# A grouped 3x3 convolution on one core: weight masks made between the first and second load issue, first loads in half images, later ones in whole images

## The chip, the cores and the metric

The kernel runs on one core of a Trainium2 chip. The metric is the device time of one execution in microseconds (us); of several executions the median counts. TensorE is PE in the profile, its weight load PEld, VectorE DVE, ScalarE ACT, GpSimd POOL, SyncE SP. Sixteen DMA engines move data between HBM and the core.

## The reference

x is float32 of 16 images, 64 channels, 64x64 pixels. The 64 input channels fall into 8 groups of 8, the 128 output channels into 8 groups of 16, and a 3x3 kernel with a border of zeros runs within each group. The output is float32, 16 x 128 x 64 x 64.

```python
x_pad = np.pad(x, ((0, 0), (0, 0), (pad, pad), (pad, pad)), mode='constant')
for g in range(groups):
    for b in range(batch):
        for co in range(c_out_per_group):
            for ci in range(c_in_per_group):
                for kh in range(k):
                    for kw in range(k):
                        output[b, g * c_out_per_group + co] += \
                            weight[g * c_out_per_group + co, ci, kh, kw] * \
                            x_pad[b, g * c_in_per_group + ci, kh:kh+h, kw:kw+w]
```

## The kernel before

Data. x is read as 1024 rows (image, channel) of 4096 pixels. Four tiles `xn[i]` and four tiles `xs[i]`, 128 rows each, hold all of it as bf16, so that each has its own place and no load ever waits for a tile to come free. `xn[i]` starts at row 128i and holds two whole images; `xs[i]` starts at row 544 + 128i, shifted by half an image, so that 32 of its rows belong to the group before or after: 32 rows of `xs[3]` (rows 96 to 127) hold the first half of image 8 and are needed in group 0. `load` (L52 to L56) issues one DMA on GpSimd's queue that reads float32 and writes bf16. The tile framework gives the loads eight semaphores in turn, so the ninth load waits on POOL until the first has landed, the tenth until the second, and so on.

Order of the loads (L61 to L69). Group 0 (`xn[0]`, the 32 rows of `xs[3]`, `xs[0]`) comes in three cuts of image rows: 0 to 16, 16 to 32, 32 to 64. Groups 1 to 3 come in two halves of 32 image rows for `xn[i]` and `xs[i]`. These are 21 DMAs. A 128-row half is 1 MB as read, a quarter 512 KB.

Weights. `w_sb` (36 KB) is loaded on SP's queue (L59). DVE sets `mask` to one and `ident` to zero (L74, L84); POOL makes of them, by three affine selects (L75, L79, L85), the mask of 8 groups and the identity. They stand behind all loads in POOL's order. DVE multiplies `w_sb` with `mask` into `E` (L94, five instructions), PE transposes `E` by 18 matmuls with `ident` (L107), and DVE and ACT copy the results as bf16 into `wN` and `wS` (L115, L117): block-diagonal weights for 32 input channels by 64 output channels at a time.

The main loop. Four groups i, each of four images; in each, eight chunks c of 8 image rows. For a chunk, four PSUM tiles of 128 x 512 are filled by 9 taps times 8 streams, 72 matmuls of 32 rows by 64 columns (`mm`, L131), each with its own weight load; eight PSUM tiles let two chunks be open. DVE and ACT in turn copy each PSUM tile into an output tile `ob` (L161, L163). After four chunks, SP issues four stores of 1 MB (L168), one for each image's half. Sixteen `ob` tiles, so four such sets, are in use before one is written again. Chunk 3 reads one image row beyond the first half (the tap below), so chunks 0 to 2 need the first 32 rows alone.

Of the kernel before, what the change touches and what calls it, by code (L numbers as in the profile page):

```python
# [7 lines left out]
FP32 = mybir.dt.float32  # L8
BF16 = mybir.dt.bfloat16
ALU = mybir.AluOpType  # L10
# [3 lines left out]
def kernel(  # L14
# [7 lines left out]
    nc = tc.nc  # L22

    B, C, H, W = x.shape
    CO, CIg, K, _ = weight.shape
    G = groups
    COg = CO // G
# [8 lines left out]
    wpool = ctx.enter_context(tc.tile_pool(name="wpool", bufs=1))  # L36
# [9 lines left out]
    xn = [xpool.tile([128, H, W], BF16, name=f"xn{i}") for i in range(4)]  # L46
    xs = [xpool.tile([128, H, W], BF16, name=f"xs{i}") for i in range(4)]

    def flat(t):
        return t.rearrange("p h w -> p (h w)")  # L50

    def load(t, row0, p0, p1, h0, h1):  # L52
        nc.gpsimd.dma_start(  # L53
            flat(t)[p0:p1, h0 * W : h1 * W],
            xr[row0 + p0 : row0 + p1, h0 * W : h1 * W],
        )  # L56
# [1 line left out]
    w_sb = wpool.tile([128, CIg * T], FP32)  # L58
    nc.sync.dma_start(w_sb, weight.rearrange("co ci kh kw -> co (ci kh kw)"))  # L59

    cuts = [0, 16, 32, 64]  # L61
    for h0, h1 in zip(cuts, cuts[1:]):
        load(xn[0], 0, 0, 128, h0, h1)
        load(xs[3], 512 - 96, 96, 128, h0, h1)
        load(xs[0], 544, 0, 128, h0, h1)
    for i in range(1, 4):
        for h0, h1 in ((0, 32), (32, 64)):
            load(xn[i], 128 * i, 0, 128, h0, h1)
            load(xs[i], 544 + 128 * i, 0, 128 if i < 3 else 96, h0, h1)  # L69

    mask = wpool.tile([128, G], FP32)
    nc.vector.memset(mask, 1.0)  # L74
    nc.gpsimd.affine_select(  # L75
        out=mask, in_=mask, compare_op=ALU.is_ge, fill=0.0,
        base=0, channel_multiplier=1, pattern=[[-COg, G]],
    )
    nc.gpsimd.affine_select(  # L79
        out=mask, in_=mask, compare_op=ALU.is_ge, fill=0.0,  # L80
        base=COg - 1, channel_multiplier=-1, pattern=[[COg, G]],
    )
    ident = wpool.tile([128, 128], BF16)
    nc.vector.memset(ident, 0.0)  # L84
    nc.gpsimd.affine_select(  # L85
        out=ident, in_=ident, compare_op=ALU.not_equal, fill=1.0,
        base=0, channel_multiplier=1, pattern=[[-1, 128]],
    )
    E = wpool.tile([128, T, 160], BF16)
    wv = w_sb.rearrange("co (ci t) -> co t ci", t=T)  # L90
    ge = 160 // CIg
# [112 lines left out]
```

## Time and profile before

| what | us |
|---|---|
| median of 3 executions | 147.95 |
| lowest and highest | 146.76, 151.19 |
| the profiled execution | 146.28 |
| its span, first to last instruction | 144.5 |
| PE busy | 77.0 |
| DVE busy | 45.7 |
| ACT busy | 37.1 |
| POOL busy | 12.0 |

The span is what the trace shows of the profiled execution. Its mean granted TensorE clock is 0.908 of 2.4 GHz. Matmuls of different rows and columns of the array run beside each other, so a matmul's own duration is not its share of the time.

### The profile page before, as it was taken

How to read it: one execution, taken by the hardware profiler on the slowest of the kernel's cores; microseconds unless marked ns; L12 is line 12 of the kernel's file. 1: busy time of each engine (PE TensorE's matmuls, PEld its weight loads, DVE VectorE, ACT ScalarE, POOL GpSimd, SP SyncE). 2: the span in 40 equal slices, each digit the busy share in tenths (PEclk: the TensorE clock that was granted, in tenths of full speed). 3: DMA queues.
4: the chain of work that ended last, by engine and by line, in shares of the span. 5: the costliest groups of instructions: out<-in, count | busy, mean ns of one | idle time of the engine just before them, and what ended most of it. 6: DMA issues, size and time to landing. Idle time of an engine off the chain costs nothing.

```text
span 144.5 us, 4928 instructions
## 1 busy us (share of the span) xinstructions
PE 77.0 (53%) x2322; PEld 51.5 (36%) x2322; DVE 45.7 (32%) x74; ACT 37.1 (26%) x68; POOL 12.0 (8%) x28
## 2 busy tenths in 40 slices
PE   0000000049966954769792993899549499930000
PEld 0000000045733632646571672566336367620000
DVE  0000000191534526117373333355603336613000
ACT  3000000003533524214352232254503325502000
POOL 6733312300000000000000000000000000000000
PEclk9999999999999999779999699599986869999655
DMA  3999999999997996995199799749999925998991
GB/s 41 118 185 214 215 215 210 213 214 217 215 206 219 426 426 277 413 410 245 75 428 413 290 426 413 295 168 401 426 426 422 415 91 211 404 426 367 428 424 75
DMA packets 7444, 42.29 MB, mean 293 GB/s; under 512 B 992, under 2 KB 992, under 8 KB 3328
## 3 DMA queue, kind: packets, MB, share of 16 engines
q1 hardware_dynamic: 4752, 33.59, 56.0%
q0 software_dynamic: 2672, 8.39, 30.4%
q8 instruction: 18, 0.29, 0.8%
q14 instruction: 2, 0.02, 0.0%
HBM read 16.81 MB, written 33.55 MB: 348 GB/s over the span
## 4 chain that ended last, share of the span: by engine, by line
PE 53%; issue 17%; DMA 16%; DVE 2%; POOL 2%; DVEq 0%; POOLq 0%
PE ps L131 52%; DMA xs<-in_x_dram 11%; DMA xn<-in_x_dram 5%; DVE E L94 2%; PE ps L107 1%; POOL xn L53 1%; POOL xs L53 1%; DVE ob L163 0%; DVEq L199 0%; POOL ident L85 0%; POOL mask L75 0%; POOLq L199 0%; POOLq L75 0%; POOLq L185 0%
## 5 line engine op out<-in xcount | busy, mean ns | idle before, releaser
L131 PE MATMUL ps<-xs,wS 32*64 32x504 bf16 (+3 forms) x1152 | 73.7, 412 | 22.6 <-issue 22.4
L131 PE MATMUL ps<-xn,wN 32*64 32x504 bf16 (+3 forms) x1152 | 74.9, 413 | 0.0
L163 DVE COPY ob<-ps 128x512 f32<-128x512 f32 x64 | 41.2, 686 | 57.5 <-PE ps L131 57.5
L131 PEld LDWEIGHTS <-wS 32*64 32x64 bf16 x1152 | 47.3, 115 | 18.6 <-issue 3.1
L161 ACT COPY ob<-ps 128x512 f32<-128x512 f32 x64 | 34.6, 589 | 63.1 <-PE ps L131 54.3
L131 PEld LDWEIGHTS <-wN 32*64 32x64 bf16 x1152 | 40.3, 115 | 29.1 <-issue 27.8
L107 PE MATMUL ps<-ident,E 128*128 128x128 bf16 x18 | 2.1, 313 | 30.8 <-DVE E L94 30.8
L107 PEld LDWEIGHTS <-E 128*128 128x128 bf16 x18 | 1.8, 147 | 30.8 <-DVE E L94 30.8
L94 DVE TENSOR_TENSOR E<-w_sb,mask 128x288 bf16<-128x288 f32 x5 | 2.9, 643 | 27.4 <-POOL mask L79 27.4
L117 ACT CAST wS<-ps 128x512 bf16<-128x512 f32 (+1 forms) x3 | 1.2, 487 | 30.3 <-PE ps L107 30.3
L53 POOL DMA_DIRECT2D xs<-in_x_dram x12 | 6.4, 536 | 9.9 <-DMA xs<-in_x_dram 7.3
L53 POOL DMA_DIRECT2D xn<-in_x_dram x9 | 5.0, 550 | 6.0 <-DMA xn<-in_x_dram 4.6
L115 DVE CAST wN<-ps 128x512 bf16<-128x512 f32 (+1 forms) x3 | 1.5, 551 | 0.1
L117 ACT ACT_TABLE_LOAD x1 | 1.3, 1283 | 0.8 <-PEq L185 0.8
L74 DVE MEMSET mask<- 128x8 f32 x1 | 0.1, 65 | 0.9 <-PEq L185 0.9
L85 POOL TENSOR_SCALAR_AFFINE_SELECT ident<-ident 128x128 bf16<-128x128 bf16 x1 | 0.3, 298 | 0.0
L75 POOL TENSOR_SCALAR_AFFINE_SELECT mask<-mask 128x8 f32<-128x8 f32 x1 | 0.2, 204 | 0.1
L79 POOL TENSOR_SCALAR_AFFINE_SELECT mask<-mask 128x8 f32<-128x8 f32 x1 | 0.2, 191 | 0.0
L185 POOL MEMSET const-float32-0.0<- 128x1 f32 x1 | 0.1, 99 | 0.3 <-issue 0.3
L84 DVE MEMSET ident<- 128x64 uint32 x1 | 0.1, 112 | 0.0
L185 POOL MEMSET const-bfloat16-1.0<- 128x1 bf16 x1 | 0.1, 102 | 0.0
L185 POOL MEMSET const-uint8-127<- 128x1 uint8 x1 | 0.1, 102 | 0.0
(1 smaller groups left out, 0.1 us busy)
## 6 DMA issues: line engine op xcount, KB each, us to landing
out_dram<-ob SPq DMA_DIRECT2D x32, 1024.0 KB, 8.8
xn<-in_x_dram POOLq DMA_DIRECT2D x7, 512.0 KB, 17.6
xs<-in_x_dram POOLq DMA_DIRECT2D x5, 512.0 KB, 16.2
xs<-in_x_dram POOLq DMA_DIRECT2D x2, 384.0 KB, 19.4
xn<-in_x_dram POOLq DMA_DIRECT2D x2, 256.0 KB, 5.8
xs<-in_x_dram POOLq DMA_DIRECT2D x2, 256.0 KB, 6.9
xs<-in_x_dram POOLq DMA_DIRECT2D x2, 64.0 KB, 5.7
xs<-in_x_dram POOLq DMA_DIRECT2D x1, 128.0 KB, 9.5
```

Of the source, the lines that this page charges most:

```text
L53: nc.gpsimd.dma_start(flat(t)[p0:p1, h0 * W : h1 * W], xr[row0 + p0 : row0 + p1, h0 * W : h1 * W],)
L75: nc.gpsimd.affine_select(out=mask, in_=mask, compare_op=ALU.is_ge, fill=0.0, base=0, channel_multiplier=1, pattern=[[-COg, G]],)
L79: nc.gpsimd.affine_select(out=mask, in_=mask, compare_op=ALU.is_ge, fill=0.0, base=COg - 1, channel_multiplier=-1, pattern=[[COg, G]],)
L85: nc.gpsimd.affine_select(out=ident, in_=ident, compare_op=ALU.not_equal, fill=1.0, base=0, channel_multiplier=1, pattern=[[-1, 128]],)
L94: nc.vector.tensor_mul(E[:, :, 32 * r : 32 * r + 32].rearrange("p t (g c) -> p t g c", c=CIg), wv.unsqueeze(2).to_broadcast([128, T, 4, CIg]),
L107: nc.tensor.matmul(ps[:, 128 * t : 128 * t + 128], E[:, t0 + t, off : off + 128], ident, start=True, stop=True,)
L115: nc.vector.tensor_copy(dst, ps[:, 0 : 128 * n])
L117: nc.scalar.copy(dst, ps[:, 0 : 128 * n])
L131: nc.tensor.matmul(d3[64 * half : 64 * half + 64, o0 : o0 + nr, v0 : v0 + nw], wt[32 * q : 32 * q + 32, 3 * kh + kw, 64 * half : 64 * half ...
L161: nc.scalar.copy(dst, pcs[b])
L163: nc.vector.tensor_copy(dst, pcs[b])
L185: nc = _bacc.Bacc("TRN2", target_bir_lowering=False, num_devices=1)
```

## The change

The masks' memsets and the three selects move up. POOL now issues the first load, runs the selects, and then issues the other loads. Group 0 comes in two halves instead of three cuts, with `xs[0]` before the piece of `xs[3]`; groups 1 to 3 come as whole images, one DMA for each tile. There are 12 loads instead of 21. All that follows (`E`, the transposes, the main loop, the stores) is the same.

```diff
-    cuts = [0, 16, 32, 64]
-    for h0, h1 in zip(cuts, cuts[1:]):
+    mask = wpool.tile([128, G], FP32)
+    ident = wpool.tile([128, 128], BF16)
+    nc.vector.memset(mask, 1.0)
+    nc.vector.memset(ident, 0.0)
+
+    def make_masks():
+        nc.gpsimd.affine_select(
+            out=mask, in_=mask, compare_op=ALU.is_ge, fill=0.0,
+            base=0, channel_multiplier=1, pattern=[[-COg, G]],
+        )
...
+    for h0, h1 in ((0, 32), (32, 64)):
         load(xn[0], 0, 0, 128, h0, h1)
+        if h0 == 0:
+            make_masks()
+        load(xs[0], 544, 0, 128, h0, h1)
         load(xs[3], 512 - 96, 96, 128, h0, h1)
-        load(xs[0], 544, 0, 128, h0, h1)
     for i in range(1, 4):
-        for h0, h1 in ((0, 32), (32, 64)):
-            load(xn[i], 128 * i, 0, 128, h0, h1)
-            load(xs[i], 544 + 128 * i, 0, 128 if i < 3 else 96, h0, h1)
...
-    nc.gpsimd.affine_select(
...
+        load(xn[i], 128 * i, 0, 128, 0, H)
+        load(xs[i], 544 + 128 * i, 0, 128 if i < 3 else 96, 0, H)
```

POOL before, the last loads and what follows them (names carry a running number; DMASW0 to DMASW7 are the semaphores of the loads):

```order
L53 DMA xn3_70<-in_x_dram 128x2048 [waits DMASW3_49]
L53 DMA xs3_74<-in_x_dram 96x2048 [waits DMASW4_49]
L75 ISA
L75 AFFINE_SELECT mask_98<-mask_98 128x8 [waits DVE_49]
L85 AFFINE_SELECT ident_102<-ident_102 128x128 [waits DVE_49]
L79 AFFINE_SELECT mask_98<-mask_98 128x8 [waits Pool_49]
L199 UNCONDITIONAL_BRANCH
```

POOL of the changed kernel, from the first load to the second that waits:

```order
L53 DMA xn0_67<-in_x_dram 128x2048
L67 ISA
L67 AFFINE_SELECT mask_77<-mask_77 128x8 [waits DVE_49]
L75 AFFINE_SELECT ident_78<-ident_78 128x128 [waits DVE_49]
L71 AFFINE_SELECT mask_77<-mask_77 128x8 [waits Pool_49]
L53 DMA xs0_71<-in_x_dram 128x2048
L53 DMA xs3_74<-in_x_dram 32x2048
L53 DMA xn0_67<-in_x_dram 128x2048
L53 DMA xs0_71<-in_x_dram 128x2048
L53 DMA xs3_74<-in_x_dram 32x2048
L53 DMA xn1_68<-in_x_dram 128x4096
L53 DMA xs1_72<-in_x_dram 128x4096
```

The selects stood behind 21 loads, 13 of which wait for an earlier one to land; now one load stands ahead of them, and it waits for none.

PE before, at chunk 3 of group 1, where the matmuls first touch the second half of `xn[1]` and `xs[1]` (PE's first matmul of the group, further up, waits for the first half, DMASW1 and DMASW2):

```order
L131 MATMUL ps_1047<-xs0_71,wS_114 64x8x63
L131 LDWEIGHTS wN_113
L131 MATMUL ps_1045<-xn1_68,wN_113 64x8x63 [waits DMASW3_49]
L131 LDWEIGHTS wS_114
L131 MATMUL ps_1047<-xs1_72,wS_114 64x8x63 [waits DMASW4_49]
```

PE of the changed kernel at the beginning of group 1:

```order
L134 MATMUL ps_710<-xs3_74,wS_105 64x7x63
L134 LDWEIGHTS wN_104 [waits DMASW6_49]
L134 MATMUL ps_796<-xn1_68,wN_104 64x512 [waits Activation_49]
L134 LDWEIGHTS wS_105 [waits DMASW7_49]
L134 MATMUL ps_798<-xs1_72,wS_105 64x512 [waits DVE_49]
```

The waits of chunk 3 are gone, and the group's first matmuls wait for the whole tiles, the seventh and eighth load (DMASW6, DMASW7). PE's instructions are otherwise the same, 4646 in both.

## Rows read from the trace of the kernel before

**Rows 1.** The page: busy tenths in 40 slices of the span, and GB/s.
```profile
PE   0000000049966954769792993899549499930000
...
DMA  3999999999997996995199799749999925998991
GB/s 41 118 185 214 215 215 210 213 214 217 215 206 219 426 426 277 413 410 245 75 428 413 290 426 413 295 168 401 426 426 422 415 91 211 404 426 367 428 424 75
```

**Rows 2.** Chain of waits: start us, us, what; the first row by engine.
```profile
PE 53%; issue 17%; DMA 16%; DVE 2%; POOL 2%; DVEq 0%; POOLq 0%
...
28.40 2.32 DVE E L94 x4
...
41.91 3.66 PE ps L131 x128
...
47.01 3.66 PE ps L131 x128
...
58.58 5.29 PE ps L131 x128
...
65.05 3.66 PE ps L131 x128
...
69.60 7.12 PE ps L131 x256
...
130.34 0.68 DVE ob L163
```

**Rows 3.** Timeline of POOL and SP: start us, us, instruction, idle before it.
```profile
0.81 0.38 SPq L59 DMA_DIRECT2D w_sb<-in_weight_dram  x1
1.29 0.67 POOL L53 DMA_DIRECT2D xn<-in_x_dram  x1 [0.78 <-POOLq L185]
...
27.18 0.52 POOL L53 DMA_DIRECT2D xs<-in_x_dram  x1 [1.93 <-DMA xs<-in_x_dram]
27.79 0.20 POOL L75 TENSOR_SCALAR_AFFINE_SELECT mask<-mask 128x8 f32<-128x8 f32 x1
...
28.18 0.19 POOL L79 TENSOR_SCALAR_AFFINE_SELECT mask<-mask 128x8 f32<-128x8 f32 x1
...
44.94 89.98 SPq L168 DMA_DIRECT2D out_dram<-ob  x32
```

**Rows 4.** Timeline of PE from 30 us.
```profile
30.77 2.10 PE L107 MATMUL ps<-ident,E 128*128 128x128 bf16 x18 [30.77 <-DVE E L94]
...
33.98 0.63 PE L131 MATMUL ps<-xs,wS 32*64 32x512 bf16 x2
```

**Rows 5.** Busy time by stretch, with PEclk, DMA share, GB/s at the end.
```profile
48.90:53.00 4.10, 2.39 (x95) 1.50 (x80) 1.77 (x3) 1.16 (x3) 0.00 (x0) 1.00 1.02 424
68.40:70.80 2.40, 1.51 (x64) 0.90 (x55) 0.65 (x2) 0.51 (x2) 0.00 (x0) 1.00 0.03 10
...
142.80:144.55 1.75, 0.00 (x0) 0.00 (x0) 0.00 (x0) 0.00 (x0) 0.00 (x0) 0.50 0.00 0
```

**Rows 6.** DMA queues: packets, MB, share; the page, then 44.8:45.8, 50:51, 62.6:63.6.
```profile
q8 instruction: 18, 0.29, 0.8%
...
HBM read 16.81 MB, written 33.55 MB: 348 GB/s over the span
...
q8 instruction: 1, 0.02, 6.0%
...
q8 instruction: 1, 0.02, 5.5%
...
q8 instruction: 1, 0.02, 5.8%
```

**Rows 7.** DMA issues, KB as written, us to landing; the last row: stores (tile ob).
```profile
xn<-in_x_dram POOLq DMA_DIRECT2D x2, 256.0 KB, 5.8
...
w_sb<-in_weight_dram SPq DMA_DIRECT2D x1, 36.0 KB, 1.9
...
DMA to landing us min/median/max: 4.2/8.8/12.1
```

More of the change, by code (lines that the diff above doesn't have):

```diff
@@ L59 @@
     nc.sync.dma_start(w_sb, weight.rearrange("co ci kh kw -> co (ci kh kw)"))
-    cuts = [0, 16, 32, 64]
-    for h0, h1 in zip(cuts, cuts[1:]):
+    mask = wpool.tile([128, G], FP32)
[7 more added lines that the diff above has]
+        )
+        nc.gpsimd.affine_select(
+            out=mask, in_=mask, compare_op=ALU.is_ge, fill=0.0,
+            base=COg - 1, channel_multiplier=-1, pattern=[[COg, G]],
+        )
+        nc.gpsimd.affine_select(
+            out=ident, in_=ident, compare_op=ALU.not_equal, fill=1.0,
+            base=0, channel_multiplier=1, pattern=[[-1, 128]],
+        )
+    for h0, h1 in ((0, 32), (32, 64)):
         load(xn[0], 0, 0, 128, h0, h1)
+        if h0 == 0:
+            make_masks()
+        load(xs[0], 544, 0, 128, h0, h1)
         load(xs[3], 512 - 96, 96, 128, h0, h1)
-        load(xs[0], 544, 0, 128, h0, h1)
     for i in range(1, 4):
-        for h0, h1 in ((0, 32), (32, 64)):
-            load(xn[i], 128 * i, 0, 128, h0, h1)
-            load(xs[i], 544 + 128 * i, 0, 128 if i < 3 else 96, h0, h1)
-    mask = wpool.tile([128, G], FP32)
-    nc.vector.memset(mask, 1.0)
-    nc.gpsimd.affine_select(
[L76 to L88, printed above, removed]
+        load(xn[i], 128 * i, 0, 128, 0, H)
+        load(xs[i], 544 + 128 * i, 0, 128 if i < 3 else 96, 0, H)
     E = wpool.tile([128, T, 160], BF16)
```

## The prediction

> **What bounds the kernel now.** I read the page's busy shares and its forty slices first [rows 1], then the chain of waits in order of time [rows 2], then POOL's and the first PE instructions [rows 3, 4], and last the DMA engines by stretch and queue [rows 5 to 7].
>
> The slices fall into two phases [rows 1]. Through the first eight slices PE does nothing while the DMA row stands at 9; after that PE works and the DMA row has holes. The span is 144.5 us, the profiled execution took 146.28 us, so 1.78 us lie around the span; the median of the three runs, 147.95 us, is 1.67 us above that execution. I sum against 146.28.
>
> Why PE idles to 30.77 us: POOL issues the loads and also makes the masks, and the masks come last. From the ninth load on, each issue waits for an earlier load to land (1.93 us at the last one); the last load goes out at 27.18 us, the three mask instructions run from 27.79 to 28.37, DVE starts E at 28.40 and PE its first matmul at 30.77 [rows 3, 4]. The weights and the first images were there long before: loads of 256 KB as written, 512 KB as read, landed 5.8 us after issue [rows 7].
>
> Why PE then takes from 33.98 us (the first matmul on xs, where the stream becomes dense [rows 4]) to 130.34 us [rows 2]: 128 matmuls in a row take 3.66 us, then comes a gap (1.44 us from 41.91 + 3.66 = 45.57 to 47.01) that the chain gives to "issue", 17% of the span in all, so nothing that the profile shows released it [rows 2]. The step of 128 tells what is missing: 128 matmuls and 128 weight loads are 256 instructions, and the instruction queue moved 18 packets of 0.29 MB in all, 16 KB each [rows 6], which is 64 bytes for each of 256. So PE waits for its next block of program. The places agree: a whole instruction packet (5.5 to 6.0% of 16 engines' 1 us, about 0.9 us) lies in 44.8:45.8, in 50:51 and in 62.6:63.6 [rows 6], and PE resumes at 47.01 and 65.05 [rows 2], 1.2 and 1.5 us behind the first and the last of these stretches. With the DMA busy, the packet in 50:51 begins 3.0 us after the resumption at 47.01 and that in 62.6:63.6 begins 4.0 us after the one at 58.58. Where the DMA is nearly idle (68.4:70.8, share 0.03 [rows 5]) the next block boundary has no gap: 256 matmuls run in one piece from 69.60 [rows 2]. From 41.91 to 69.60 are five such cycles, 5.54 us each; the whole dense stage is 96.4 us for 18 blocks, 5.35 each. The program supply, slowed by data transfers, paces PE; PE paces the stores; the DMA idles at times.
>
> The DMA's own floor: stores run at 424 GB/s, loads show 214 because what is written is half of what is read [rows 1, 5], so both move some 426 GB/s at their wider end. 16.81 MB read and 33.55 MB written [rows 6] are then 39.4 + 78.8 = 118.2 us; one 1 MB load or store is 2.46 us.
>
> **The change, part by part.** Masks: the three POOL instructions, 0.6 us, move from behind 21 loads to behind the first one. The first issue ends at 1.29 + 0.67 = 1.96 us [rows 3], the masks at about 2.65; the weight load lands at 0.81 + 1.9 = 2.7 us [rows 3, 7]. E's 2.32 us of lead [rows 2] then end at 5.0 us, PE can begin at 5.1, and its first matmul on images, behind the 2.10 us of weight matmuls [rows 4], at 7.2. The memsets that the masks need stay DVE's first instructions. The 0.6 us by which the second load is later costs nothing: the first load, now 1 MB, gives the DMA 2.46 us of work.
>
> What is late next is the data: two 1 MB halves and the quarter piece, 2.46 + 2.46 + 0.62 = 5.5 us from about 2.6 us on, where the DMA starts (the first slice of 3.6 us is 0.3 busy [rows 1]), so 8.1 us. A landing adds to that; the shortest store took 4.2 us for 2.46 us of transfer [rows 7], so 0 to 1.7, and I take 0.9. The dense stream begins at 9.0 us instead of 33.98: **25.0 us earlier**. If all behind it kept its pace, the span would be 119.5 us.
>
> Whole images instead of halves: PE now waits at the first chunk of group 1 for all of both tiles, not half. Group 0 is 11.1 us of loads, to 13.7; group 1 adds 9.84, to 23.5 us alone. PE comes to group 1 after 576 matmuls, 4.5 cycles of 5.54 us, at 9 + 25 = 34 us. The stores begin (first issue 44.94 [rows 3], 11.0 us after the dense start) at 20.0 us and halve the rate for the rest, so group 1 lands near 28. Group 2 at half rate lands at 48, wanted at 59 or later; group 3 at 66, wanted at 84. Cost nothing; with only a third of the rate for loads group 3 lands near 88, so up to 4 us. The two row cuts in group 0 merge with no wait: chunk 3 needs the second half at about 19 us, it lands at 14.5. Fewer, larger DMAs also take the slow start away (118 and 185 GB/s in the second and third slice, 214 after [rows 1]): some 2 us less DMA time, free unless the DMA bounds.
>
> What it gives back: loads and stores now overlap, which no stretch of before shows; the stores began at 44.94 us [rows 3], and GB/s goes there from the loads' 214 to the stores' 426 within two slices [rows 1]. At 20.0 us, 17.4 of the loads' 39.4 us are done and 22.0 left; at half the rate that is 44 us, at two thirds 33; I take 38.5 us of mixed traffic. In it a program block has two data queues to get past. Bounds for its extra wait: 0 (the wait is the same with one queue or two) and 4.92 us (one whole-image load of 2 MB at full rate, ahead of it each time). I take 2.46 us, one 1 MB transfer, since the waits seen with one queue, 3.0 and 4.0 us, are of that size. Cycle 5.54 + 2.46 = 8.0 us, 38.5/8.0 = 4.8 cycles, **11.8 us later**. Upper bound: 44/10.46 = 4.2 cycles, 20.7 us. Below nothing I see no way, as the DMA is never emptier than before.
>
> A rule bears on this by itself. The Trainium skill, DMA: Bandwidth & Descriptors, section Queues, rings and completion order, says that each DMA engine takes its queues in turn and drains a whole packet, typically 9 to 17 descriptors, before it switches. By that rule a second busy queue adds one turn to each fetch; its size for whole images would be the upper bound above, and the span 119.5 + 20.7 + 2.1 = 142.3 us. The 3.0 and 4.0 us measured beside one queue fit a turn of about 2.5 us, and no row here has two.
>
> After the loads the DMA is backlogged all the time, with no idle stretch such as 68.4:70.8 in which a block comes in time. I charge the five-cycle mean instead of the stage's: 0.19 us for each of about 11 cycles, **2.1 us**.
>
> Sum: 144.5 - 25.0 + 11.8 + 2.1 = 133.4 us of span, 135.2 us with the 1.78 around it. Check against the DMA: 2.6 + 118.2 + 1.7 (the empty end, 142.8 to 144.5 [rows 5]) = 122.5 us, so PE and its program still bound, by 11 us, and the end stays as it is, four stores behind PE's last matmul.
>
> **The rivals.** (a) The program fetch is not slowed by a second queue: 119.5 + 2.1 is under the DMA's 122.5, so the DMA bounds, 122.5 to 127 us of span, 124 to 129 us. For it: a packet's own 0.9 us is the same as the loads end (44.8:45.8) and amid stores (62.6:63.6) [rows 6]. Against: the gap goes where the DMA empties. A rule of the Trainium skill ends here too: Runtime: NRT & Kernel Launch, section Instruction fetch mechanics, has the crossing of a 16 KiB program block mostly hidden. By it PE would run through and the DMA's floor would decide; the gaps in the chain, 17% of the span, speak against it.
>
> (b) Each fetch waits for whole-image loads, the upper bound: 119.5 + 20.7 + 2.1 = 142.3, minus what a PE that stalls gives back (fewer stores, so the loads end sooner): 138 to 142 us, 140 to 144 with what lies around. The large packets speak for it.
>
> (c) Slower: loads and stores in flight together run at a lower joint rate. About 44 us of DMA work (22 of loads, as much of stores) is mixed. The time passes 150.9 us, 2% over 147.95, when the span passes 149.1, 26.6 over the floor: 44/r - 44 = 26.6, r = 0.62, some 265 GB/s together. From there it decides; at r = 0.6 the span is 151.8, 153.6 us with the rest. Nothing in the trace has the two together, for or against; stores alone reach 424 and loads, counted as read, 428.
>
> (d) Hardly any gain (145 to 151 us): r near 0.66, or loads that get so little of the DMA that groups 2 and 3 starve PE by 10 us on top of (b). That the masks don't come early is no case: the order of POOL's instructions shows them second.
>
> **How the numbers follow.** Forecast (129 to 140) 0.52, (a) 0.22, (b) 0.16, (d) 0.06, (c) 0.04. The range 126 to 143 leaves out the lower part of (a), (c), (d) and the end of (b), 2 in 10. A measurement of this kernel tells about 2%; faster by more than that means under 145.0: 0.90 from the forecast, (a) and (b). Within 2%: 0.06. Slower: 0.04.
>
> **What would show it.** Right: masks done before 3 us, first matmul near 5, dense stream near 9; program gaps longer between 20 and 60 us (cycles near 8 us) than after; group boundaries with no wait on DMA; PE's last matmul 13 us before the end. Wrong: a DMA row full from start to end with GB/s at 426 (then a), a joint rate clearly under 400 while both queues are busy (c or d), matmuls released by xn or xs at group 2 or 3, or cycles of 8 us that go on after the loads.

## The result, and the profile after

| | before | after |
|---|---|---|
| median, us | 147.35 (4 runs) | 132.66 (4 runs, 132.49 to 132.89) |
| profiled execution, us | 146.28 | 132.79 |
| its span, us | 144.5 | 131.1 |

The ratio of after to before is 0.900, 95% interval 0.894 to 0.906. The forecast was 135.2 us, within 126 to 143.

The head of the program, as the timeline of the changed kernel has it (start us, us, instruction), from POOL, DVE and PE:

```profile
1.30 0.66 POOL L53 DMA_DIRECT2D xn<-in_x_dram  x1 [0.79 <-POOLq L188]
2.05 0.21 POOL L67 TENSOR_SCALAR_AFFINE_SELECT mask<-mask 128x8 f32<-128x8 f32 x1
...
2.44 0.19 POOL L71 TENSOR_SCALAR_AFFINE_SELECT mask<-mask 128x8 f32<-128x8 f32 x1
...
2.75 2.88 DVE L97 TENSOR_TENSOR E<-w_sb,mask 128x288 bf16<-128x288 f32 x5 [1.72 <-DMA w_sb<-in_weight_dram]
...
5.12 2.10 PE L110 MATMUL ps<-ident,E 128*128 128x128 bf16 x18 [5.12 <-DVE E L97]
7.21 2.98 PE L134 MATMUL ps<-xn,wN 32*64 32x512 bf16 x13
10.13 0.64 PE L134 MATMUL ps<-xs,wS 32*64 32x512 bf16 x2
```

Against [rows 3, 4]: the masks end at 2.63 us instead of 28.37, and E now waits for the weight load. PE's stream gets dense at 10.13 us instead of 33.98, 23.85 us earlier. The page's slices, beside [rows 1]:

```profile
PE   0499997497546556587919884759749289340000
...
DMA  3999999999999999999999999999999729989991
GB/s 31 173 209 211 230 210 223 200 293 273 290 280 295 270 295 268 395 423 420 425 415 428 420 415 423 428 420 418 400 415 420 295 118 420 423 343 393 435 423 48
```

The holes of the DMA row are gone but for one, at 104 to 107 us. PE's row has more of them. The chain of waits (start us, us, what), beside [rows 2]:

```profile
24.80 5.35 PE ps L134 x128
...
30.99 3.56 PE ps L134 x119
...
37.74 3.61 PE ps L134 x128
...
43.93 3.66 PE ps L134 x128
...
50.40 3.66 PE ps L134 x128
...
56.32 5.25 PE ps L134 x124
...
98.60 3.66 PE ps L134 x128
102.26 3.08 issue
105.34 7.12 PE ps L134 x256
...
116.90 0.68 DVE ob L166
```

Stretches (duration, then busy us of each engine; the last two numbers are the DMA share and GB/s), and the two data queues while both run, in 28:48 (packets, MB, share):

```profile
24.80:50.40 25.60, 16.18 (x512) 10.95 (x512) 9.02 (x14) 7.62 (x14) 0.00 (x0) 0.93 1.02 279
56.32:104.00 47.68, 33.96 (x1024) 22.05 (x1024) 18.05 (x28) 15.13 (x28) 0.00 (x0) 0.89 1.00 415
104.00:106.70 2.70, 1.36 (x56) 1.00 (x63) 0.52 (x1) 0.67 (x2) 0.00 (x0) 1.00 0.23 85
```

```profile
q0 software_dynamic: 383, 2.79, 66.6%
q1 hardware_dynamic: 389, 2.82, 34.8%
```

So the span went from 144.5 to 131.1 us in three terms. The start came 23.85 us earlier. The dense stage got longer, from 96.4 to 106.8 us (10.13 to 116.90): 10.4 us given back. Behind PE's last matmul stand 14.2 us, as before. What the stage pays is the cycle of 128 matmuls, one program block: 5.35 us on average before; now 6.40 while loads and stores overlap (four cycles from 24.80 to 50.40) and 6.13 under stores alone (eight from 56.32 to 105.34). The queue rows say that the overlap itself is cheap: 2.79 MB written are 5.58 MB read, so 8.4 MB moved in 20 us, 420 GB/s, close to either alone [rows 1, 5].

Neither the clock nor the matmuls set the length of these cycles. Two stretches of PE, and the program packet (queue q8) that begins in 41.6:41.7:

```profile
24.80:30.14 5.34, 5.34 (x128) 3.37 (x128) 1.95 (x4) 1.89 (x4) 0.00 (x0) 0.68 0.96 264
...
37.74:41.35 3.61, 3.61 (x128) 2.76 (x128) 1.29 (x2) 1.07 (x2) 0.00 (x0) 1.00 1.03 281
```

```profile
q8 instruction: 1, 0.02, 58.4%
```

In the first the granted clock was 0.68 on average, part of it at 1.2 GHz, behind 2.81 us in which PE had no matmul. In the second it was at 2.4 GHz. The 128 matmuls took 5.34 and 3.61 us, the gaps behind them 0.85 and 2.58 us, and both cycles are 6.19 us long (24.80 to 30.99, 37.74 to 43.93). The packet begins 3.9 us after PE resumed at 37.74, takes 0.93 us (58.4% of 16 engines' 0.1 us), and PE goes on 1.4 us behind its end.

### The profile page after: what moved, and what is told of

Its sections match the earlier page's. It is cut to its first block, busy times and chain, and to the rows that moved or that the text cites. A ratio compares the mean times of both kernels' runs of the same rounds, so it can differ in the third digit from the quotient of the medians.

```text
span 131.1 us, 4919 instructions
## 1 busy us (share of the span) xinstructions
PE 79.4 (61%) x2322; PEld 52.4 (40%) x2322; DVE 45.8 (35%) x74; ACT 37.1 (28%) x68; POOL 7.2 (6%) x19
## 4 chain that ended last, share of the span: by engine, by line
PE 61%; issue 25%; DVE 2%; DMA 1%; DVEq 0%
PE ps L134 59%; DVE E L97 2%; PE ps L110 2%; DMA w_sb<-in_weight_dram 1%; DVE ob L166 1%; DVEq L202 0%; DVEq L97 0%
## 5 line engine op out<-in xcount | busy, mean ns | idle before, releaser
L134 PE MATMUL ps<-xn,wN 32*64 32x504 bf16 (+3 forms) x1152 | 77.3, 413 | 0.0
L134 PEld LDWEIGHTS <-wN 32*64 32x64 bf16 x1152 | 40.9, 114 | 39.4 <-issue 38.5
L53 POOL DMA_DIRECT2D xs<-in_x_dram x7 | 3.7, 531 | 4.2 <-DMA xs<-in_x_dram 2.4
L53 POOL DMA_DIRECT2D xn<-in_x_dram x5 | 2.8, 570 | 1.9 <-DMA xn<-in_x_dram 1.1
```

What stands on the lines that cost most here:

```text
L53: nc.gpsimd.dma_start(flat(t)[p0:p1, h0 * W : h1 * W], xr[row0 + p0 : row0 + p1, h0 * W : h1 * W],)
L134: nc.tensor.matmul(d3[64 * half : 64 * half + 64, o0 : o0 + nr, v0 : v0 + nw], wt[32 * q : 32 * q + 32, 3 * kh + kw, 64 * half : 64 * half ...
```

## The experiments

Eleven kernels, all cut from the changed one. Ratios are against the kernel before on the same chip. Four were executed once each: small stores, program doubled, group 0 only, seven taps.

### Which part of the change carries it

Masks alone: the loads are those of before.

```diff
-    for h0, h1 in ((0, 32), (32, 64)):
+    cuts = [0, 16, 32, 64]
+    for h0, h1 in zip(cuts, cuts[1:]):
         load(xn[0], 0, 0, 128, h0, h1)
         if h0 == 0:
             make_masks()
...
-        load(xn[i], 128 * i, 0, 128, 0, H)
+        for h0, h1 in ((0, 32), (32, 64)):
+            load(xn[i], 128 * i, 0, 128, h0, h1)
...
```

> The masks move up as in the change, the loads stay those of before (three cuts, then halves). Theory 1, the masks' place carries the gain: first matmul near 5 us, dense stream between 8 and 11 us, time 130 to 136 us, within 2% of the changed kernel's 132.7. Theory 2, the load shapes carry a good part of it: 137 us or more. On the way: if packets of a whole image make a program block wait longer than packets of a half, the cycles of 128 matmuls while loads and stores overlap are shorter here than the 6.3 us of the changed kernel.

Measured: 132.87 us, ratio 0.901 (0.894 to 0.908), the changed kernel's own. Theory 1 holds: the place of the masks carries the gain. The side guess on packet size did not come true. The cycles in the overlap are 6.5 us (22.94, 29.41, 35.88, 42.62, 49.09 in its chain), not shorter with half images. In 28:48 its queues read:

```profile
q1 hardware_dynamic: 575, 4.19, 52.0%
q0 software_dynamic: 571, 2.07, 51.1%
```

The two queues move as many packets each, 575 and 571 here, 389 and 383 with whole images. A packet here is one row. A load's row is twice as large there, so loads get 66.6% of the DMA in place of 51.1%. That decides when the loads end (near 54 us or near 71), and nothing came of it, since no group was late in either kernel.

Loads alone: the masks behind the twelve loads.

```diff
         load(xn[0], 0, 0, 128, h0, h1)
-        if h0 == 0:
-            make_masks()
...
         load(xs[i], 544 + 128 * i, 0, 128 if i < 3 else 96, 0, H)
+    make_masks()
```

> The loads of the change, the masks behind all of them. With 12 loads POOL gets through its queue sooner: in the changed kernel the last load goes out at 13.2 us, so the masks end near 14.5, the first matmul comes near 17 and the dense stream near 20 us, some 10 us later than with the change, 14 us earlier than before. Theory 1 (the start of PE's stream sets the end): 138 to 142 us. Theory 2 (the DMA's total work sets the end, the start matters little): 131 to 135 us. Theory 3 (load shapes bring nothing): 147 us.

Measured: 139.12 us, ratio 0.944 (0.933 to 0.955), theory 1. The masks ran at 13.41 us, the dense stream began at 19.61. Fewer loads let POOL through its queue sooner, and that alone brings 5.6%; with the masks in front the shape of the loads adds nothing. The end comes 6.1 us of span later than with the change for a start 9.5 us later; the rest is made up on the way, by cycles that get shorter where the DMA runs dry.

### Is it the program supply, and what slows it

The transfers taken away: each store writes 128 of 2048 columns.

```diff
-                    nc.sync.dma_start(outf[imgs[b]][:, s0 : s0 + HALF], obs[b])
+                    nc.sync.dma_start(outf[imgs[b]][:, s0 : s0 + 128], obs[b][:, 0:128])
```

> As the changed kernel, but each store writes 128 of its 2048 columns: most of the output stays unwritten. The DMA is then nearly idle from the end of the loads, near 43 us, on. Theory 1, transfers delay PE's program: after that point the gaps at every 128 matmuls go, cycles fall from 6.2 to 3.7 to 4.3 us, PE ends at 80 to 92 us and the span is 84 to 96 us. Theory 2, the gaps belong to PE (evictions, PSUM tiles, the block size itself): cycles stay at 6 us, PE ends near 115 and the span is near 118 us.

Measured: span 92.2 us. Its chain, at the end of the loads and after, and its page's DMA row:

```profile
37.45 3.61 PE ps L134 x128
41.06 2.86 issue
43.92 3.66 PE ps L134 x128
47.58 0.34 issue
47.92 3.66 PE ps L134 x128
51.59 0.07 issue
51.65 3.66 PE ps L134 x128
```

```profile
DMA  0899999999999999999810210022013004000300
```

As long as the loads run, a cycle takes 6.3 us with this one queue busy; from their end, near 46 us, it takes 3.68 (eleven cycles from 47.92 to 88.39 in its chain). Theory 1: transfers, not PE, make the gaps.

The program doubled: matmuls of 256 columns.

```diff
...
-            for k, (kh, kw) in enumerate(taps):
-                for b, wt, xt, q, half in streams:
-                    mm(pcs[b], wt, xt, q, half, c, kh, kw, k == 0, k == T - 1)
+            for r0 in (0, R // 2):
+                for k, (kh, kw) in enumerate(taps):
+                    for b, wt, xt, q, half in streams:
+                        mm(pcs[b], wt, xt, q, half, c, r0, kh, kw, k == 0, k == T - 1)
```

> As the changed kernel, but each matmul of 512 columns is cut into two of 256: the same columns, products and transfers, twice the instructions on PE (some 9250). Theory 1, the program supply paces PE at some 6.1 us for 128 matmuls under a busy DMA and 3.7 us at best: the dense stage has 36 blocks and takes 130 us or more (at 3.7 us) to 220 us (at 6.1 us); I expect 150 to 190 us, as the stores come more slowly and leave the DMA idle more often. Theory 2, PE is paced by its columns, its evictions or the DMA: 130 to 140 us.

Measured: 199.8 us, with the same columns; the dense stage takes 174 us, theory 1. 128 matmuls now take 1.96 us, and the wait behind them is longer by what they are shorter (two neighbours of its chain, then the program packet that begins in 161.9:162.0):

```profile
160.81 1.96 PE ps L135 x128
162.76 1.77 issue
164.54 1.96 PE ps L135 x128
```

```profile
q8 instruction: 1, 0.02, 74.3%
```

This one cycle is 3.73 us, with the DMA nearly dry (share 0.19): what is counted is instructions, not columns. Its packet begins 1.1 us after PE resumed, takes 1.2 us, and PE goes on 1.4 us behind its end. In the changed kernel's cycle from 37.74 us these were 3.9, 0.9 and 1.4 us, so what a busy DMA adds lies ahead of the packet. And even with the DMA dry the supply takes 3.7 us a block: it keeps up with 128 matmuls of 512 columns, 3.66 us, and no more.

One queue instead of two: the loads of groups 1 to 3 left out.

```diff
-    for i in range(1, 4):
-        load(xn[i], 128 * i, 0, 128, 0, H)
...
-            (0, wN, xn[i], 0, 0), (2, wS, xs[i], 0, 1),
+            (0, wN, xn[0], 0, 0), (2, wS, xs[0], 0, 1),
...
```

> As the changed kernel, but the loads of groups 1 to 3 are left out and all groups compute on group 0's tiles: from 14 us on the stores are alone on the DMA, which has 11 us of loads and 79 us of stores. Theory 1, a second busy queue adds to the wait for a program block: the cycles between 22 and 52 us, 6.3 us in the changed kernel, fall by 1 to 2.5 us. Theory 2, it is a busy DMA as such, one queue or two: cycles stay at 6.0 to 6.4 us wherever stores run without a break, and fall only behind stretches in which the DMA runs dry; span 118 to 124 us, because such stretches are more frequent, as before the change (5.35 us on average).

Measured: span 120.7 us, theory 2. With stores alone its cycles between 27 and 47 us stay at 6.4:

```profile
27.47 5.22 PE ps L131 x119
32.69 1.25 issue
33.94 3.61 PE ps L131 x128
37.55 2.58 issue
40.13 5.35 PE ps L131 x128
45.48 1.12 issue
46.60 3.66 PE ps L131 x128
```

So loads alone cost 6.3 us a cycle, stores alone 6.1 to 6.4, both 6.4 (6.5 with half images). A second busy queue adds at most some 0.4 us.

### What bounds the changed kernel

Shorter program, same bytes: two of the nine taps left out.

```diff
-            for k, (kh, kw) in enumerate(taps):
+            for k, (kh, kw) in enumerate(taps[:7]):
...
```

> As the changed kernel, but two of the nine taps are left out, which takes 22% of PE's matmuls and program (3622 instructions in place of 4646) and no byte of the transfers. If PE's program supply sets the end, PE ends some 23 us sooner and the span falls until the DMA's own work sets it, 124 to 127 us. If PE is free of it already and the DMA's backlog sets the end of the changed kernel, the span stays at 129 to 131 us.

Measured: span 128.1 us. PE ended 20.5 us sooner, the span 3.0. Its page's rows and two stretches:

```profile
PE   0499989097929592919293859858380000000000
...
DMA  2999999999999999999999999999999999999950
```

```profile
2.60:122.00 119.40, 66.36 (x1810) 40.98 (x1810) 45.66 (x72) 35.80 (x67) 5.82 (x12) 0.85 1.02 348
122.00:126.10 4.10, 0.00 (x0) 0.00 (x0) 0.00 (x0) 0.00 (x0) 0.00 (x0) 0.50 0.37 158
```

Here the DMA never waits for PE. The changed kernel stands 3.0 us above that: the dry stretch at 104 to 106.7 (share 0.23, so 2.1 us) and a thin one while the last stores wait for PE. The expectation named 124 to 127 and 129 to 131 and got a value between: the DMA all but sets the changed kernel's end, at 128 and not at 122.5 us.

Can a version beat it? Five kernels cut stores into smaller pieces, to shorten the 14.2 us tail and to learn whether a program block waits for a whole transfer. They store n chunks at a time, n = 4 being the change. The edit of the one that cuts only the last four chunks:

```diff
-            if c % 4 == 3:
-                s0 = HALF * (c // 4)
+            last = i == 3 and c >= 4
+            n = 1 if last else 4
+            if c % n == n - 1:
+                s0 = R * W * (c - n + 1)
+                o0 = 512 * (c % 4 - n + 1)
                 for b in range(4):
-                    nc.sync.dma_start(outf[imgs[b]][:, s0 : s0 + HALF], obs[b])
+                    nc.sync.dma_start(
+                        outf[imgs[b]][:, s0 : s0 + 512 * n],
+                        obs[b][:, o0 : o0 + 512 * n],
+                    )
```

All stores with n = 1 (256 KB):

> As the changed kernel, but each chunk's four 256 KB are stored at once, 128 stores in place of 32. Theory 1, a program block waits behind the transfer that is under way (2.46 us for 1 MB): with 0.6 us transfers the cycles under stores fall from 6.1 to about 4.5 us and PE ends before 105 us. Theory 2, the wait belongs to a busy DMA, whatever the size of the transfers: cycles stay at 6.0 to 6.3 us, PE ends near 117 us, and only the tail gets shorter, from 14 us behind PE's last matmul to 4 to 7 us: span 121 to 125 us, 123 to 127 us of time.

All with n = 2 (512 KB):

> As the run before, with stores of 512 KB after every second chunk, 64 in all. Theory 1: cycles of about 5 us. Theory 2: cycles of 6.0 to 6.3 us, tail 7 to 9 us behind PE's last matmul, 126 to 129 us of time.

Measured: 138.09 us (0.939, 0.932 to 0.946) and 134.65 us (0.915, 0.910 to 0.921), both slower than the changed kernel, and above every time that was expected of them. With 512 KB the cycles are 5.9 us against 6.13, so the wait hardly shrinks with the transfer: theory 2 on that. With 256 KB PE did end sooner, at 101.8 us, with cycles of 4 to 5.7 us after the loads, but the DMA moved only 365 GB/s in 54:100 and stayed busy for 33 us more. Its stretch of three cycles just after the loads, and its queues in 28:46:

```profile
59.52:75.09 15.57, 10.83 (x384) 7.23 (x384) 6.44 (x10) 5.37 (x10) 0.00 (x0) 1.00 1.04 395
```

```profile
q0 software_dynamic: 456, 3.34, 88.8%
q1 hardware_dynamic: 458, 0.83, 13.7%
```

In 59.52:75.09 the DMA is full (share 1.04) and a cycle takes 5.19 us, so here the smaller stores shorten it, by some 0.9 us against 6.13; the cycles of 4.0 to 4.6 us come later, where the DMA has gaps. Packet for packet again, so stores of 2 KB rows get 13.7% of the DMA while loads run. The 512 KB run shows a third thing, at its end:

```profile
50.00:123.00 73.00, 47.37 (x1458) 30.44 (x1435) 27.07 (x42) 22.64 (x42) 0.00 (x0) 0.87 1.02 412
...
127.00:131.30 4.30, 0.00 (x0) 0.00 (x0) 0.00 (x0) 0.00 (x0) 0.00 (x0) 0.50 0.06 26
```

For its last 4.3 us a share of 0.06, one engine of sixteen, works alone at 26 GB/s. The sixteen don't finish together. PE's blocks, 18 of 0.9 us, may all have gone through that one; no run tests it.

Only the last four chunks with n = 1, the others as in the change:

> As the changed kernel, but the last four chunks are stored one by one in 256 KB pieces; all other stores stay 1 MB. If PE and its program set the end, with the DMA ready to take stores as they come (it ran dry at 104 to 107 us in the changed kernel), then only the tail behind PE's last matmul shrinks, from 14.2 us to 5 to 7 us: span 121 to 125 us, time 123 to 127 us. If the DMA's backlog sets the end, as in the runs that cut all stores, nothing is gained: 131 to 134 us.

With n = 2:

> The same with 512 KB pieces for the last four chunks. If PE sets the end: tail of 8 to 9 us, span 124 to 127 us, time 126 to 129 us, 2 to 3 us behind the run with 256 KB pieces. If the DMA's backlog does: 131 to 134 us.

The whole last group, n = 2 and then 1:

> As the changed kernel, but all of the last group is stored in smaller pieces: 512 KB after every second chunk up to chunk 3, 256 KB after each of the last four. The runs that cut only the last four chunks kept a dry stretch of the DMA near 104 us (some 2 to 3 us of idle) and a tail of 2 to 3 us in which about one DMA engine works. If the dry stretch can be filled by storing earlier: 130 to 131.5 us, 1 to 2% under the changed kernel. If the DMA was to move the same bytes at the same rate anyway: 132 to 134 us.

Measured: 132.87 us (0.892, 0.884 to 0.900), 132.88 us (0.891, 0.883 to 0.899) and 134.01 us (0.918, 0.914 to 0.923). None beats the change clear of the intervals, and the third is slower clear of them. In the first, PE ended 1.9 us sooner and the span by 0.3: the tail behind PE did not shrink, as the DMA still had the set before to store. In the third the dry stretch near 104 us is gone (share 1.01 in 104:106.7), and the time is 1% longer all the same. The theory that PE sets the end falls in all three, as it does with the seven taps.

## Why the prediction was right

**The start, "25.0 us earlier": right.** The masks ended at 2.63 us (2.65 predicted), PE began at 5.12 (5.1), the images' first matmul came at 7.21 (7.2). The dense stream came at 10.13 instead of 9.0: it stood 2.0 us behind the 8.1 us of transfers, not the 0.9 taken.

**"Whole images instead of halves ... cost nothing": right.** No wait of PE for a load of groups 1 to 3 is in the list of waits, and the run with halves has the same time.

**"In it a program block has two data queues to get past ... 11.8 us later": wrong in its cause.** This step charged the second queue with one 1 MB transfer, 2.46 us, in every cycle. A busy DMA costs a cycle of 6.1 to 6.5 us whichever queue keeps it busy; the overlap's own share is at most 0.27 us (6.40 against 6.13) for each of about five cycles, some 1.3 us in place of 11.8. The size of both terms together came out near because the next one was too small in turn, which is luck.

**"After the loads the DMA is backlogged all the time ... 2.1 us": right in kind, mis-sized.** The five cycles that I took for a busy DMA, 5.54 us, had the dry stretch near 68 us among them. Unbroken, a cycle is 6.13. Of the 10.4 us by which the stage grew, the rest, some 9, is put down to this. Both terms together were 13.9 us against 10.4: that is the 2.3 us by which the span was over, with 1.2 us of the start against it.

How long a turn is, the rows of 28:48 tell. Each queue moves one packet for one of the other, and a packet is one row: on average it held its engine for 0.56 us (a load: 66.6% of 16 engines' 20 us, by 383) or 0.29 us (a store). The records of the trace agree: a row of one queue begins at the end of nearly every row of the other. So a turn of the second queue is worth 0.3 to 0.6 us and not 2.46, and the 0.27 us measured can't tell such a turn from none. The Trainium skill (DMA: Bandwidth & Descriptors, Queues, rings and completion order) says that a DMA engine takes its queues in turn, a packet at a time. The equal counts, 389 and 383, agree with it; its size of a turn, 9 to 17 descriptors, is not told by the rows here.

**"PE and its program still bound, by 11 us, and the end stays as it is": wrong, by 8 us.** With 22% less program the span fell by 3.0 us only. The floor of 122.5 us was too low, as the seven taps show part by part: 49.7 MB by 122 us are 416 GB/s, not 426 (2.7 us), and the last 0.65 MB take 4.1 us at a share of 0.37 where a full DMA takes 1.5 (2.6 us). So PE, slowed by its program, and the DMA ran nearly level, and the time is close to where either puts it; that the forecast held with PE as the bound owes something to this. The DMA row that is full nearly to the end is what the text had given as the sign for rival (a); as to the program fetch, (a) was the better account, with the wrong floor.

**The rivals.** Against (b): at most 0.4 us per cycle and not 4.92. Against (c) and (d): 420 GB/s with both queues busy. The Trainium skill (Runtime: NRT & Kernel Launch, Instruction fetch mechanics) has the crossing of a program block mostly hidden. The trace agrees where the DMA is idle and the matmuls have 512 columns, 3.68 us for 3.66 us of matmuls. It does not with 256 columns, 3.73 us for 1.96, nor where the DMA is busy, 6.1 to 6.5.

## What to carry to other kernels

Small set-up work behind a queue of DMA issues on the same engine starts when that queue has drained, not when its data is there: put it behind the first issue. A gap at every 128 matmuls that nothing releases is PE's next program block; in this kernel it shows whenever the DMA is busy. Cutting the same matmuls in two cost 67 us (199.8 against 132.66). The price of a block is read from cycles with an unbroken DMA. Before working on the tail of an engine, take some of its work away and see whether the end moves at all.

## What the runs showed that I had not expected

The wait for a program block hardly depends on which transfers run: loads, stores, both, pieces of 512 KB or 1 MB, all give 5.9 to 6.5 us a cycle, against 3.68 with the DMA idle; only pieces of 256 KB gave less, 5.2. What the busy DMA adds is time before the program packet begins, 3.9 us after PE resumed against 1.1 with the DMA dry. What holds the packet back that long stays open: a row or two of 0.3 to 0.6 us ahead of it would not do it. Two queues share the DMA by packets, one for one (456 and 458, with bytes, counted as read, 8 to 1), so the shape of a transfer sets its share. And storing in finer pieces made the kernel slower, 134.65 and 138.09 us against 132.66, where the DMA was already the bound.
